# Longer runs of one operand type in split float32 products, and the rounded copies on another engine

## The chip, the cores and the metric

The kernel runs on one core of a Trainium2 chip. The metric is the device time of one execution in microseconds. TensorE (PE in the profile) multiplies, and its weight loads (PEld) have rows of their own; VectorE (DVE), ScalarE (ACT) and GpSimd (POOL) work on tiles, each with an in-order queue; SyncE (SP) issues most transfers (DMA).

## The reference: what is computed

Two decoder layers over 1024 tokens of width 1024, each with a residual and a layer normalization behind it. One input projection per layer gives four groups of columns: main, memory queries, main gate, memory gate.

```python
def mixer_sublayer(x, mem, w_in, w_mem_kv, w_out, main_fn):
    h = x @ w_in
    u_main = h[..., :D_MAIN]            # 1024 columns
    q_mem = h[..., D_MAIN:D_MIX]        # 512 columns, 4 heads of 128
    g_main = h[..., D_MIX:D_MIX + D_MAIN]
    g_mem = h[..., D_MIX + D_MAIN:]
    y_main = main_fn(u_main)
    y_mem = memory_attention(q_mem, mem, w_mem_kv)
    y = concatenate([y_main * silu(g_main), y_mem * silu(g_mem)])
    return y @ w_out
# per layer: x = layer_norm(ALPHA * x + mixer_sublayer(...))
```

In the first layer `main_fn` is a causal pooling with windows of 2, 4, 8 and 16 tokens, followed by a 256x256 matrix for each of four groups. Between the layers one projection of `x` gives keys, values and forget gates. In the second layer `main_fn` is the forgetting attention: 16 heads of 64, logits plus a difference of cumulated log gates, causal softmax. `memory_attention` is an attention with 4 heads over 256 memory tokens. All is float32.

## The kernel before

**The split.** A float32 matrix `a` is kept in three parts: `hi`, `a` rounded to float32r; `lo`, the rest `a - hi` in bfloat16; and `top`, `a` rounded to bfloat16. A product of `a` and `b` is the sum of three products into one accumulator, given by `three` (L153): `hi*hi` in float32r (the profile writes f32), `top*lo` and `lo*top` in bfloat16. `hi_lo` (L156) makes the parts: ScalarE casts `hi` (L159), VectorE subtracts for `lo` (L160), GpSimd copies `top` (L161). Inside the forgetting attention (`low[0]` is true) the weights' three parts are all made by GpSimd (`gp_hi_lo`, L163). `split_w` (L168) issues a weight piece's load on SP and splits it.

**The stages, in time.** The input `X` is loaded transposed and split (`load_x`, L493). Then layer 0: pooling group 0, `mem_kv(0)`, `mem_attention(0)`, pooling groups 1 to 3 (`pool_group`, L521) with parts of the output projection's weights split in between, then the output projection `OutProj.rest` (L436) with the normalization `norm` (L460), which turns each row tile by TensorE transposes (L277) into the next `X`. Layer 1: `mem_kv(1)`, whose projections have those transposes spread between them (`spread`), `mem_attention(1)`, the first pairs' keys, queries and values (`v_first`, L622), the forgetting attention `fox` with projections filled in between its own products, then `OutProj.rest` again.

**Where products are ordered.** `slab` (L193) is the projection of 128 columns for all 1024 tokens: two accumulators (token halves `n`) and two weight pieces `pc` of four 128-row blocks each, 48 products of 512 columns. It is a generator that yields after each product; some are run at once, and others are handed to a `Fill`, which pumps as many columns of them as fit between a stage's own products. `project` in `mem_kv` makes 24 products of 256 columns. The memory attention's `probs` makes three products of 256 columns for each head and row tile. `pool_group` multiplies with the 256x256 matrix. `products` (L413) of `OutProj` makes, for two row tiles `a` and two column halves `nh`, groups of twelve products, for each third `c` of the rows of `w_out`. `v_first` makes 24 products of 272 columns for a row tile. In all of them the innermost loops take the four (or one) float32r products of a piece and then its eight (or two) bfloat16 ones. The order on TensorE is the program's order within `manual_schedule` and is set by the tile scheduler by readiness elsewhere; on the other engines the scheduler sets it, but for instructions marked `keep_in_program_order`.

**Buffers.** Weight pieces rotate through six buffers `w` (two for a piece: `hi`, and `lo` with `top`), raw weights through four `raw`. Slabs accumulate in two banks `pj`; output projections in `pj`, `L`, `T` and `O`. An accumulator is emptied by ScalarE and VectorE: `gate` (L216) by a tanh on ScalarE and a product on VectorE, others by a copy or cast on ScalarE.

Of the kernel before, what the change touches and what calls it, by code (L numbers as in the profile page):

```python
# [18 lines left out]
P = 128  # L19
# [4 lines left out]
NH = 512  # L24
# [48 lines left out]
def trunk_kernel(ctx, tc, x, xT, memT, win, wk, wv0, wv, wmk, wmv, wout, poolw, pscale, lng, lnb, bforget, out):  # L73
# [79 lines left out]
    def three(a, b):  # L153
        return (a.hi, b.hi), (a.top, b.lo), (a.lo, b.top)

    def hi_lo(to, src, pinned=False, top=None):  # L156

        pin = tc.keep_in_program_order if pinned else lambda ins: ins
        pin(nc.scalar.copy(to.hi, src))  # L159
        pin(nc.vector.tensor_tensor(to.lo, src, to.hi.bitcast(F32), ALU.subtract))  # L160
        nc.gpsimd.tensor_scalar(to.top, to.hi.bitcast(F32) if top is None else top, 1.0, 1.0, ALU.mult, ALU.mult)  # L161

    def gp_hi_lo(to, src):  # L163
        nc.gpsimd.tensor_scalar(to.hi, src, 1.0, 1.0, ALU.mult, ALU.mult)
        nc.gpsimd.tensor_tensor(to.lo, src, to.hi.bitcast(F32), ALU.subtract)  # L165
        nc.gpsimd.tensor_scalar(to.top, src, 1.0, 1.0, ALU.mult, ALU.mult)

    def split_w(src_dram, shape):  # L168
        r = raw(shape)
        nc.sync.dma_start(r, src_dram)  # L170
        to = parts_of(wt, shape)
        if low[0]:
            gp_hi_lo(to, r)
        else:
            hi_lo(to, r, top=r)
        return to
# [16 lines left out]
    def slab(pieces_dram, X, evac, banks=("pj", 2)):  # L193

        arrived = isinstance(pieces_dram, list)
        ws = list(pieces_dram) if arrived else [split_w(pieces_dram[0], [P, 4, P])]
        accs = {}
        for n, pc in ((0, 0), (1, 0), (0, 1), (1, 1)) if arrived else ((0, 0), (0, 1), (1, 0), (1, 1)):
            if len(ws) <= pc:
                ws.append(split_w(pieces_dram[pc], [P, 4, P]))  # L200
            if n not in accs:
                accs[n] = ps([P, NH], *banks)
            for i, (a, b) in enumerate(three(ws[pc], X)):
                for k in range(4):
                    kt = pc * 4 + k
                    nc.tensor.matmul(  # L206
                        accs[n], a[:, k, :], b[:, kt, n * NH : (n + 1) * NH],
                        start=kt == 0 and i == 0, stop=kt == KT - 1 and i == 2,
                    )
                    if kt == KT - 1 and i == 2:  # L210
                        evac(slice(n * NH, (n + 1) * NH), accs[n])
                    yield NH
# [8 lines left out]
    def mem_kv(l):  # L221

        ms = [parts_of(T, [P, 4, NMEM]) for _ in range(2)]
        for q in range(4):
            r = raw([P, 2, NMEM])
            nc.sync.dma_start(r, memT[:, 2 * q : 2 * q + 2, :])
            hi_lo(ms[q // 2][:, 2 * (q % 2) : 2 * (q % 2) + 2, :], r, top=r)
        mk = parts_of(MK, [P, MH, NMEM])

        def project(w_dram):  # L230

            acc = ps([P, NH], "pj", 2)[:, :NMEM]
            for pc in range(2):
                for i, (w, m) in enumerate(three(split_w(w_dram[pc], [P, 4, P]), ms[pc])):
                    for k in range(4):
                        nc.tensor.matmul(
                            acc, w[:, k, :], m[:, k, :],
                            start=pc == 0 and k == 0 and i == 0, stop=pc == 1 and k == 3 and i == 2,
                        )
                    if i:  # L240
                        spread()
            return acc
# [54 lines left out]
    def mem_attention(l, X, kv, qtile, ytile, yd):  # L297
# [20 lines left out]
        def probs(i):  # L318
# [54 lines left out]
    class OutProj:  # L373
# [23 lines left out]
        def split(self, upto, pinned=False):  # L397

            while self.n < upto:
                self.fetch(self.n + 1)  # L400
                n = self.n
                kk, nh, j = self.KKS[n // 4], n // 2 % 2, n % 2
                if j == 0:
                    self.ws[nh][kk] = self.wtile(n // 2)
                r = self.raws.pop(0)
                hi_lo(self.ws[nh][kk][j], r, pinned, top=r)
                self.n += 1
# [4 lines left out]

        def products(self, accs, c, ys):  # L413
            for a in range(2):
                for nh in range(2):
                    for i in range(3):
                        for k in range(4):
                            kt = 4 * c + k
                            y, w = three(ys[:, k, a * P : (a + 1) * P], self.ws[nh][kt // 2][kt % 2])[i]
                            nc.tensor.matmul(  # L420
                                accs[a][nh], y, w, start=kt == 8 and i == 0, stop=kt == 7 and i == 2,
                            )
                            yield NH

        def early(self, y, ys):
# [4 lines left out]
            for two in (slice(0, 2), slice(2, 4)):  # L430
                hi_lo(ys[:, two, :], y[:, two, :], True, top=y[:, two, :])
                yield
# [3 lines left out]
        def rest(self, resid, X, dst):  # L436
# [11 lines left out]
            for sp, c in order + [(sp, c) for sp in range(2, ST // 2) for c in (2, 0, 1)]:  # L448
# [3 lines left out]
                nc.sync.dma_start(src, self.yd[c, :, :, sp * 2 * P : (sp + 1) * 2 * P])  # L452
                hi_lo(ys, src, top=src)
                for k, _ in enumerate(self.products(accs[sp], c, ys)):
                    if c != 2 and k % 6 == 5:
                        spread()
# [36 lines left out]
    def load_x(kt, parts=1):  # L493
        r = T(dt=F32)
        for i in range(parts):
            cols = slice(i * S // parts, (i + 1) * S // parts)
            nc.sync.dma_start(r[:, cols], xT[kt, :, cols])
            hi_lo(X[:, kt, cols], r[:, cols], top=r[:, cols])

# [16 lines left out]
    with tc.tile_pool(name="in0", bufs=1) as in0:  # L516
# [4 lines left out]
        def pool_group(g):  # L521
            w = WINDOWS[g]
            pms = []
            for f in (2 * g, 2 * g + 1):
# [15 lines left out]
                pms.append(parts_of(T, [P, S]))  # L540
                hi_lo(pms[-1], pm, top=pm)
# [3 lines left out]
            hi_lo(w2, r, top=r)  # L545
            ys = []
# [30 lines left out]
    with tc.tile_pool(name="in1", bufs=1) as in1:  # L577
# [44 lines left out]
        def v_first():  # L622
# [3 lines left out]
            for kt in range(KT):  # L626
                r = raw([P, FW])
                nc.sync.dma_start(r, wv0[kt // 2, :, kt % 2, :])
                hi_lo(ws[kt // 4][:, kt % 4, :], r, top=r)
            for s in range(ST):  # L630
                acc = ps([P, NH], "pj", 2)
                for kt in range(KT):
                    for i, (u, w) in enumerate(three(X[:, kt, s * P : (s + 1) * P], ws[kt // 4][:, kt % 4, :])):
                        nc.tensor.matmul(acc[:, :FW], u, w, start=kt == 0 and i == 0, stop=kt == KT - 1 and i == 2)
                        yield FW
# [359 lines left out]
```

## Time and profile before

| | us |
|---|---|
| three runs, median (lowest to highest) | 1229.82 (1229.51 to 1230.13) |
| the profiled execution | 1230.34 |
| its span, first to last instruction | 1228.6 |
| TensorE busy | 1202.2 |
| VectorE busy | 839.8 |
| ScalarE busy | 567.3 |
| GpSimd busy | 415.8 |

The granted TensorE clock is 0.997 on average. The span is 1.7 us shorter than the profiled execution's time; the rest lies around it. Rows of the profile name an instruction's line, engine and operation, its output and inputs by the program's names without numbers, the shapes and types, how many were put together, and in brackets or at the end what the engine had waited for. A group's start is the recorded start of its first instruction, and products overlap, so a pitch is taken from starts. `[1.44 <-DVE A L160]` says that TensorE was idle for 1.44 us and that the wait ended with VectorE's write of `A` in line 160.

### The profile page before, as it was taken

To read this page: it belongs to the slowest core of one execution; us is meant where nothing else is said; L and a number is where in the kernel's file an instruction comes from. 1 tells how busy PE (TensorE), PEld (TensorE's weight loads), DVE (VectorE), ACT (ScalarE), POOL (GpSimd) and SP (SyncE) were. 2 spreads that over 40 slices of the span, in tenths; PEclk is the share of its full clock that TensorE was granted. 3 is DMA by queue.
4 is the path that set the end of the run, shared out by engine and by line. 5 is a ranking of instruction groups with operands and counts; after the bars stand their busy time and mean duration, and the time that the engine had idled before them with its cause. 6 is when DMAs were issued, how large, how long until landed. Compare 5 with 4: busy or idle time off the path is not lost. (4 is left out here: it accounts for less than half of the span.)

```text
span 1228.6 us, 20280 instructions
## 1 busy us (share of the span) xinstructions
PE 1202.2 (98%) x7018; PEld 731.9 (60%) x7018; DVE 839.8 (68%) x1853; ACT 567.3 (46%) x1241; POOL 415.8 (34%) x582
## 2 busy tenths in 40 slices
PE   8999999999999999999999999999999999999997
PEld 3566666554555556666675666566666666655553
DVE  7555777585745568457736887878877887775754
ACT  4333662242321123346423776767776777662110
POOL 7233102151421225320203454544445434573110
PEclk9999999999999999999999999999999999999999
DMA  6233544223452334234517778878787989885430
GB/s 223 86 108 93 136 106 144 103 87 112 128 207 103 105 111 154 69 103 100 156 48 185 159 164 187 190 176 184 176 203 165 192 182 228 214 227 180 172 120 35
DMA packets 267414, 178.68 MB, mean 145 GB/s; under 512 B 212272, under 2 KB 225712, under 8 KB 267312
## 3 DMA queue, kind: packets, MB, share of 16 engines
q1 hardware_dynamic: 267312, 177.40, 54.1%
q8 instruction: 55, 0.90, 0.3%
q14 instruction: 47, 0.39, 0.1%
HBM read 94.97 MB, written 22.61 MB: 96 GB/s over the span
## 5 line engine op out<-in xcount | busy, mean ns | idle before, releaser
L206 PE MATMUL pj<-A,w 128*128 128x512 bf16 (+1 forms) x2928 | 691.8, 399 | 7.1 <-DVE A L160 2.0
L206 PEld LDWEIGHTS <-w 128*128 128x128 bf16 x1984 | 170.3, 98 | 236.1 <-issue 65.8
L206 PEld LDWEIGHTS pj<-A,w 128*128 128x128 f32 x976 | 179.2, 189 | 56.1 <-ACT A L159 3.9
L161 POOL TENSOR_SCALAR w<-raw 128x512 bf16<-128x512 f32 x106 | 75.3, 712 | 255.5 <-PE pj L206 163.7
L160 DVE TENSOR_TENSOR w<-raw,w 128x512 bf16<-128x512 f32 x106 | 101.5, 960 | 60.7 <-PE pj L206 43.3
L786 DVE SCALAR_TENSOR_TENSOR P<-T,s,P 128x512 f16<-128x512 f32 x192 | 111.4, 612 | 33.4 <-ACT P L785 32.1
L764 ACT ACTIVATE T<-MK,s 128x512 f32<-128x512 f32 x192 | 111.3, 579 | 43.6 <-DVE s L756 23.4
L785 ACT ACTIVATE P<-T,s 128x512 f16<-128x512 f32 x192 | 103.0, 576 | 43.7 <-ACT T L764 20.7
L420 PEld LDWEIGHTS <-T 128*128 128x128 bf16 x736 | 64.6, 98 | 88.2 <-issue 24.2
L191 PE MATMUL L<-B,B 128*128 128x512 f32 (+3 forms) x384 | 106.2, 383 | 1.1 <-DVE s L756 1.1
L159 ACT CAST w<-raw 128x512 fp32r<-128x512 f32 x106 | 65.3, 618 | 72.0 <-PE pj L206 39.3
L748 POOL TENSOR_SCALAR_AFFINE_SELECT R<-R 128x128 f32<-128x128 f32 x128 | 41.8, 332 | 162.8 <-DVE s L756 127.2
L191 PEld LDWEIGHTS L<-B,B 128*128 128x128 f32 x384 | 71.0, 189 | 21.6 <-DVE s L756 2.6
L756 DVE CUSTOM_DVE_ANT_0 MK<-L,R 128x512 f32<-128x512 f32 (+3 forms) x128 | 72.4, 566 | 11.5 <-PE L L191 7.9
L165 POOL TENSOR_TENSOR w<-raw,w 128x512 bf16<-128x512 f32 x54 | 69.7, 1292 | 25.4 <-PE pj L206 25.1
L161 POOL TENSOR_SCALAR T<-T 128x1024 bf16<-128x1024 f32 x23 | 31.1, 1353 | 123.4 <-PE pj L420 79.3
L159 ACT CAST T<-T 128x1024 fp32r<-128x1024 f32 x23 | 24.0, 1046 | 103.3 <-DMA T<-y0d 53.5
L160 DVE TENSOR_TENSOR T<-T,T 128x1024 bf16<-128x1024 f32 x23 | 34.2, 1487 | 43.2 <-PE pj L420 24.3
L808 PE MATMUL O<-T,V 128*64 128x128 f16 (+1 forms) x1152 | 57.6, 221 | 2.0 <-DMA T<-P 1.9
L808 PEld LDWEIGHTS <-V 128*64 128x64 f16 (+1 forms) x1152 | 50.0, 104 | 15.1 <-issue 7.9
L420 PE MATMUL pj<-B,T 128*128 128x512 bf16 (+1 forms) x192 | 54.4, 399 | 0.0
L420 PE MATMUL L<-B,T 128*128 128x512 f32 (+1 forms) x168 | 48.0, 405 | 1.2 <-POOL T L161 1.2
(230 smaller groups left out, 1748.8 us busy)
## 6 DMA issues: line engine op xcount, KB each, us to landing
raw<-in_win_dram SPq DMA_DIRECT2D x96, 256.0 KB, 2.7
raw<-in_wout_dram SPq DMA_DIRECT2D x40, 256.0 KB, 2.8
B<-B SPq DMA_DIRECT2D x32, 256.0 KB, 4.1
R<-cumd SPq DMA_DIRECT2D x16, 512.0 KB, 4.7
y0d<-Y SPq DMA_DIRECT2D x12, 512.0 KB, 2.9
T<-y0d SPq DMA_DIRECT2D x12, 512.0 KB, 3.8
T<-y1d SPq DMA_DIRECT2D x11, 512.0 KB, 3.9
raw<-in_wmk_dram SPq DMA_DIRECT2D x16, 256.0 KB, 2.6
```

The source lines that it names most:

```text
L159: pin(nc.scalar.copy(to.hi, src))
L160: pin(nc.vector.tensor_tensor(to.lo, src, to.hi.bitcast(F32), ALU.subtract))
L161: nc.gpsimd.tensor_scalar(to.top, to.hi.bitcast(F32) if top is None else top, 1.0, 1.0, ALU.mult, ALU.mult)
L165: nc.gpsimd.tensor_tensor(to.lo, src, to.hi.bitcast(F32), ALU.subtract)
L191: nc.tensor.matmul(acc, a, b, start=i == 0, stop=i == len(terms) - 1)
L206: nc.tensor.matmul(accs[n], a[:, k, :], b[:, kt, n * NH : (n + 1) * NH], start=kt == 0 and i == 0, stop=kt == KT - 1 and i == 2,)
L420: nc.tensor.matmul(accs[a][nh], y, w, start=kt == 8 and i == 0, stop=kt == 7 and i == 2,)
L756: nc.vector.tensor_tensor_reduce(p[:, lo:up], lg, R[:, lo:up], 1.0, top, ALU.add, ALU.min, m[:, n : n + 1])
L764: nc.scalar.activation(e, p[:, lo:up], AF.Exp, bias=top, scale=-1.0, accum_out=sums[:, n, hd % 2, i : i + 1],)
L785: nc.scalar.activation(pair[:, lo:up], e, AF.Copy, scale=r)
L786: nc.vector.scalar_tensor_tensor(pair[:, L + lo : L + up], e, r, pair[:, lo:up], ALU.mult, ALU.subtract)
L808: nc.tensor.matmul(acc[rows, (i % 4) * P : (i % 4) * P + P], v[:, b, 2 * j : 2 * j + (1 if e else 2), :].rearrange("p e d -> p (e d)"), pt ...
```

## The change

The order of products changes so that products of one operand type follow each other in longer runs. In `slab` a half's float32r products of both pieces come in one run of 8, then its 16 bfloat16 ones; the second half takes bfloat16 first, then float32r, so that a run goes on from one half to the next, and from one slab to the next. Where both pieces have arrived (the first pool group) the order goes by pieces. `project` does the same over both pieces and alternates from one call to the next; `v_first` alternates from one row tile to the next over all eight blocks; the memory logits take two heads together; the pooling's small products and the output projection's groups are ordered by type, except the very last group, which is ordered by row tile. Secondly, `hi_lo` makes `top` by a ScalarE copy, with GpSimd kept for the input `X` and for the parts of the output projection that are split inside the forgetting attention (`pinned`, `early`). The weights of the forgetting attention stay on GpSimd.

```diff
+    def gp_copy(to, src):
+        nc.gpsimd.tensor_scalar(to, src, 1.0, 1.0, ALU.mult, ALU.mult)
     def hi_lo(to, src, pinned=False, top=None):
         pin = tc.keep_in_program_order if pinned else lambda ins: ins
         pin(nc.scalar.copy(to.hi, src))
         pin(nc.vector.tensor_tensor(to.lo, src, to.hi.bitcast(F32), ALU.subtract))
-        nc.gpsimd.tensor_scalar(to.top, to.hi.bitcast(F32) if top is None else top, 1.0, 1.0, ALU.mult, ALU.mult)
+        (top or nc.scalar.copy)(to.top, src)
...
# slab
-        for n, pc in ((0, 0), (1, 0), (0, 1), (1, 1)) if arrived else ((0, 0), (0, 1), (1, 0), (1, 1)):
+        high, low_top = (0,), (1, 2)
+        if arrived:
+            order = [(n, pc, part) for pc in range(2) for n, part in ((0, high), (1, high), (1, low_top), (0, low_top))]
+        else:
+            order = [(0, pc, part) for part in (high, low_top) for pc in range(2)]
+            order += [(1, pc, part) for part in (low_top, high) for pc in range(2)]
+        for n, pc, part in order:
...
-            for i, (a, b) in enumerate(three(ws[pc], X)):
+            for i in part:
+                a, b = three(ws[pc], X)[i]
                 for k in range(4):
...
# project
-            for pc in range(2):
-                for i, (w, m) in enumerate(three(split_w(w_dram[pc], [P, 4, P]), ms[pc])):
+            ws = [split_w(w_dram[pc], [P, 4, P]) for pc in range(2)]
+            parts = (1, 2, 0) if len(projected) % 2 else (0, 1, 2)
+            projected.append(acc)
+            for i in parts:
+                for pc in range(2):
+                    w, m = three(ws[pc], ms[pc])[i]
                     for k in range(4):
...
-                    if i:
-                        spread()
+                        if k % 3 == 0:
+                            spread()
...
# memory logits
-                for j in range(2):
+                for n, j in ((0, 0), (0, 1), (1, 1), (2, 1), (1, 0), (2, 0)):
                     h = 2 * hp + j
-                    mm3(lg[:, j, :], three(qs[h][:, i * P : (i + 1) * P], mk[:, h, :]))
+                    a, b = three(qs[h][:, i * P : (i + 1) * P], mk[:, h, :])[n]
+                    nc.tensor.matmul(lg[:, j, :], a, b, start=(n, j) == (0, 0), stop=(n, j) == (2, 0))
...
# OutProj.products
-            for a in range(2):
-                for nh in range(2):
-                    for i in range(3):
+            if apart:
+                order = [(a, nh, part) for a in range(2) for part in (high, low_top) for nh in range(2)]
+            else:
+                order = [
+                    (a, nh, part) for part in ((low_top, high) if c == 0 else (high, low_top))
+                    for a in range(2) for nh in range(2)
+                ]
...
# pooling's matrix
-                    mm3(acc, terms)
+                    mm3(acc, terms[0::3] + terms[1::3] + terms[2::3])
...
# v_first
-                for kt in range(KT):
-                    for i, (u, w) in enumerate(three(X[:, kt, s * P : (s + 1) * P], ws[kt // 4][:, kt % 4, :])):
+                parts = (1, 2, 0) if s % 2 else (0, 1, 2)
+                for i in parts:
+                    for kt in range(KT):
```

More of the change, by code (lines that the diff above doesn't have):

```diff
@@ L171, in split_w @@
         to = parts_of(wt, shape)
[L172 to L175, printed above, removed]
+        (gp_hi_lo if low[0] else hi_lo)(to, r)
         return to
@@ L237, in project @@
                             acc, w[:, k, :], m[:, k, :],
-                            start=pc == 0 and k == 0 and i == 0, stop=pc == 1 and k == 3 and i == 2,
+                            start=(i, pc, k) == (parts[0], 0, 0), stop=(i, pc, k) == (parts[2], 1, 3),
                         )
-                    if i:
-                        spread()
+                        if k % 3 == 0:
+                            spread()
             return acc
@@ L411, in open, with products @@
             return accs[:2], accs[2:]
-        def products(self, accs, c, ys):
-            for a in range(2):
-                for nh in range(2):
-                    for i in range(3):
[L417 to L423, printed above, removed]
+        def products(self, accs, c, ys, apart=False):
+            high, low_top = (0,), (1, 2)
+            if apart:
[5 more added lines that the diff above has]
+                ]
+            for a, nh, part in order:
+                for i in part:
+                    for k in range(4):
+                        kt = 4 * c + k
+                        y, w = three(ys[:, k, a * P : (a + 1) * P], self.ws[nh][kt // 2][kt % 2])[i]
+                        nc.tensor.matmul(
+                            accs[a][nh], y, w, start=kt == 8 and i == 0, stop=kt == 7 and i == 2,
+                        )
+                        yield NH
         def early(self, y, ys):
@@ L430, in early @@
             for two in (slice(0, 2), slice(2, 4)):
-                hi_lo(ys[:, two, :], y[:, two, :], True, top=y[:, two, :])
+                hi_lo(ys[:, two, :], y[:, two, :], True, gp_copy)
                 yield
@@ L452, in rest @@
                 nc.sync.dma_start(src, self.yd[c, :, :, sp * 2 * P : (sp + 1) * 2 * P])
-                hi_lo(ys, src, top=src)
-                for k, _ in enumerate(self.products(accs[sp], c, ys)):
+                hi_lo(ys, src)
+                for k, _ in enumerate(self.products(accs[sp], c, ys, X is None and sp == ST // 2 - 1 and c == 1)):
                     if c != 2 and k % 6 == 5:
@@ L544, in pool_group @@
             w2 = parts_of(MK, [P, 2, 2 * P])
[L545 removed]
+            hi_lo(w2, r)
             ys = []
@@ L628, in v_first @@
                 nc.sync.dma_start(r, wv0[kt // 2, :, kt % 2, :])
[L629 removed]
+                hi_lo(ws[kt // 4][:, kt % 4, :], r)
             for s in range(ST):
                 acc = ps([P, NH], "pj", 2)
[L632 to L634 removed]
+                parts = (1, 2, 0) if s % 2 else (0, 1, 2)
+                for i in parts:
+                    for kt in range(KT):
+                        u, w = three(X[:, kt, s * P : (s + 1) * P], ws[kt // 4][:, kt % 4, :])[i]
+                        nc.tensor.matmul(
+                            acc[:, :FW], u, w, start=kt == 0 and i == parts[0], stop=kt == KT - 1 and i == parts[2],
+                        )
                         yield FW
```

23 lines of the change are left out of this document (12 added, 11 removed).

## The prediction

> **What bounds the kernel now.** I read the page's busy times first, then the chain that ended last, then TensorE's timeline where the chain runs, then every idle time that TensorE's timeline and the waits show. The page, its busy times and two of its groups:
>
> ```profile
> span 1228.6 us, 20280 instructions
> PE 1202.2 (98%) x7018; PEld 731.9 (60%) x7018; DVE 839.8 (68%) x1853; ACT 567.3 (46%) x1241; POOL 415.8 (34%) x582
> ...
> L161 POOL TENSOR_SCALAR w<-raw 128x512 bf16<-128x512 f32 x106 | 75.3, 712 | 255.5 <-PE pj L206 163.7
> ...
> L159 ACT CAST w<-raw 128x512 fp32r<-128x512 f32 x106 | 65.3, 618 | 72.0 <-PE pj L206 39.3
> ```
>
> TensorE is busy 98% of the span; no other engine passes 68%. The time is the sum of the products' pitches (start to start) and about 26 us without a product. So an edit can only pay by a shorter pitch or by a stall that goes, and can only cost by a new stall. The end of the chain shows the pitch; first and last of its evenly spaced groups of twelve:
>
> ```profile
> 1131.59 2.67 PE pj L420 x12
> ...
> 1211.69 2.69 PE pj L420 x12
> ```
>
> These lie 80.10 us and 30 groups apart: 2.670 us for 4 float32r and 8 bfloat16 products, nothing waited for. Inside two such groups (TensorE's timeline, pairs of products):
>
> ```profile
> 1184.39 0.59 PE L420 MATMUL L<-G,T 128*128 128x512 bf16 x2
> ...
> 1185.29 0.63 PE L420 MATMUL pj<-B,T 128*128 128x512 f32 x2
> 1185.76 0.60 PE L420 MATMUL pj<-V,T 128*128 128x512 bf16 x2
> 1186.20 0.59 PE L420 MATMUL pj<-B,T 128*128 128x512 bf16 x2
> ...
> 1187.06 0.59 PE L420 MATMUL pj<-B,T 128*128 128x512 bf16 x2
> 1187.95 0.63 PE L420 MATMUL L<-MK,T 128*128 128x512 f32 x2
> 1188.43 0.60 PE L420 MATMUL L<-B,T 128*128 128x512 bf16 x2
> 1188.87 0.59 PE L420 MATMUL L<-MK,T 128*128 128x512 bf16 x2
> ```
>
> A bfloat16 pair takes 0.43 us (twice the 0.2154 found below). From a bfloat16 pair over the first float32r pair it is 0.90 and 0.89, so that pair takes 0.47 or 0.46: coming into float32r costs nothing beside its slower pitch. The second float32r pair takes 0.47 or 0.48 and the first bfloat16 pair 0.44: the way back costs something. A longer bfloat16 run gives its pitch more sharply:
>
> ```profile
> 24.57 2.96 PE L206 MATMUL pj<-A,w 128*128 128x512 bf16 x13 [1.44 <-DVE A L160]
> 27.37 2.84 PE L206 MATMUL L<-A,w 128*128 128x512 bf16 x12
> ```
>
> 2.80 us over 13 products is 0.2154 us each. With 0.2325 for a float32r one (the mean of 0.47 and 0.46, halved), twelve are 8 x 0.2154 + 4 x 0.2325 = 2.653. Measured 2.670: 0.017 us for each return from float32r to bfloat16. The pairs alone say between 0.01 (0.47+0.44 against 0.47+0.43) and 0.03 (0.48+0.44 against 0.46+0.43).
>
> **The change part by part.** A. *The order.* The count of products stays 7,010. In the two built programs' order on TensorE the returns to bfloat16 fall from 599 to 223: 169 fewer in the projection slabs, 79 in the output projections, 60 in the first values, 48 in the small products, 24 in the memory keys and values; the fill inside the forgetting attention gains a few. 376 x 0.017 = -6.4 us; by the pairs' ends -3.8 to -11.3. A third of them lie between products of 256 or 272 columns, which I price alike. Products into and out of the float16 values products of the forgetting attention also move a little; no quoted row prices that, I take 0 and leave it to the range.
>
> B. *The rounded copies.* 233 of them go from GpSimd to ScalarE: 186 of 128x512, 31 of 128x1024, 16 small ones. At ScalarE's 0.618 for 512 elements, twice that at most for 1024, and 0.4 at a guess for the small ones, that is 115 + 38 + 6 = 159 us more: 567 to about 726 us, 59% of the span. GpSimd gives up at least 233 x 0.712 = 166 us. Neither is near TensorE's 98%, so the mean costs nothing; the cover is that ScalarE's casts of a slab's pieces run while TensorE works through 48 products (four groups, 10.7 us), and if that cover fails in a place, the cast's 0.6 us shows there. The transfers are as many; in a slab the second piece's load is issued on SP 8 products earlier, past nothing that is due sooner.
>
> C. *VectorE next to a quieter GpSimd.* Timelines of VectorE, GpSimd and TensorE at the end of a pool group:
>
> ```profile
> 268.20 0.68 DVE L160 TENSOR_TENSOR B<-raw,B 128x512 bf16<-128x512 f32 x1
> ...
> 274.69 1.09 DVE L160 TENSOR_TENSOR w<-raw,w 128x512 bf16<-128x512 f32 x1
> 275.70 2.11 DVE L160 TENSOR_TENSOR W<-raw,W 128x512 bf16<-128x512 f32 x2
> ```
> ```profile
> 273.66 2.60 POOL L161 TENSOR_SCALAR W<-raw 128x512 bf16<-128x512 f32 x2
> ```
> ```profile
> 278.46 5.63 PE L206 MATMUL pj<-A,w 128*128 128x512 f32 x24 [1.59 <-DVE Y L219]
> 288.58 1.62 PE L191 MATMUL L<-T,MK 128*128 128x512 f32 x6 [0.43 <-DVE Y L560]
> ```
>
> The same subtraction takes 0.68 alone and 1.05 to 1.09 while GpSimd copies. The three from 274.69 on take 3.20 us where 2.04 would do: that alone is 1.16 of the 1.59 us that TensorE then waits for VectorE's gating product, and the stretch before was as crowded. Both stalls end on VectorE and go: -2.0, ends 0 (ScalarE's queue, now with the copies, is late instead) and -2.0. At the head, the 1.44 us at 24.57 also waits for VectorE's subtraction of the input, which GpSimd's copies of weights slow; GpSimd keeps the input's own. I take -1.0, ends 0 and -1.4.
>
> D. *Start of the second layer's memory keys.* One row of busy times by stretch:
>
> ```profile
> 471.00:485.00 14.00, 13.19 (x108) 11.06 (x107) 13.83 (x28) 6.61 (x14) 9.88 (x13) 1.00 0.39 142
> ```
>
> Columns: length, then PE, PEld, DVE, ACT, POOL. VectorE is full, ScalarE has 6.61 us, GpSimd 13 copies. On ScalarE those are about ten at 0.6 and three of half size at 0.4: +7.2, so 13.8 of 14.0 us, in a queue that serves strictly in order transposed input, weights and keys. Both casts and copies are now needed by TensorE within the stretch. TensorE idles 0.8 there; from the queue's order in the changed program I count three places where a cast comes 1.0 to 2.3 us after the product that needs it, less what VectorE saves without GpSimd beside it: +2.5, ends 0 and +4.5.
>
> E. *Start of the last output projection.* Rows of TensorE's timeline, then of the chain:
>
> ```profile
> 1101.37 0.60 PE L420 MATMUL L<-B,T 128*128 128x512 bf16 x2 [1.19 <-POOL T L161]
> ...
> 1123.29 0.74 PE L420 MATMUL L<-R,T 128*128 128x512 f32 x2 [1.33 <-ACT T L159]
> ```
> ```profile
> 1108.87 2.03 POOL V L161 x2
> 1110.89 1.02 POOL G L161
> 1111.91 1.81 POOL G L835 x2
> ...
> 1122.19 1.05 ACT T L159
> ```
>
> The second stall is a chain over GpSimd: the gating product at 1111.91 stands behind copies of weights, its result goes out and comes back, then is cast. Without three copies (3.0 us) ahead of it the chain is early by more than 1.33: -1.3. The copy that the first stall waits for runs on ScalarE after a cast of 1.05, so about 1.0 late against 1.19; but the new order needs the copies 8 products (1.86 us) later. The last row tiles' outputs are evacuated by ScalarE, now behind copies: I keep 0.6 of that stall. -1.9 together, ends -2.5 and +2.0 (three copies of 0.62 ahead of the evacuation, with nothing gained).
>
> Sum: -6.4 - 2.0 - 1.0 + 2.5 - 1.9 = -8.8. Behind the last product (normalization on VectorE and the store) I find nothing that changes. The profiled execution took 1230.3 us, 0.5 above the median of 1229.8; it becomes 1221.5, and a median 1221.0.
>
> **The rivals.** R1, *only the order pays*: the stalls of C and E go and others of the same size come, since ScalarE serves casts, copies, evacuations and exponentials in one queue. For it: D is such a place. Against: outside D its busy share stays near two thirds. 1230.3 - 6.4 = 1223.9, median 1223.4.
>
> R2, *the change does not do what it says*: the 0.017 us belongs to each group's start, or to float32r itself, and long runs do not save it. For it: it is a difference of 0.6% of a group, got from rounded rows. Against: the two slower pairs sit exactly at the border. Then -2.4 by C to E: 1227.9, median 1227.4.
>
> R3, *slower: ScalarE's queue decides in the slabs*. A second piece's float32r cast is now needed 4 products (0.93 us) after the first's, not 12 (2.65 us). If its weight buffer is free only late, release, cast of 0.618 and the copy that stands ahead of it in the queue (0.618) exceed 0.93 by 0.3 us. There are some forty slabs outside the forgetting attention; from 8.8/40 = 0.22 us each on the gain is eaten, at 0.3 it is +12: about 1233.5. For it: the idle of the casts in the page's group ends mostly with a product (39.3 us of 72.0), so buffers are what they wait for. Against: in the changed program's order the buffer taken by the second piece is one that was released some 20 products before.
>
> R4, *slower: narrow float32r products wait for their weights in long runs*. Rows of four memory projections in the first layer and of their weight loads:
>
> ```profile
> 71.29 5.80 PE L236 MATMUL pj<-T,w 128*128 128x256 f32 x48
> 76.84 2.48 PE L206 MATMUL pj<-A,w 128*128 128x512 f32 x10
> ```
> ```profile
> L236 PEld LDWEIGHTS pj<-T,w 128*128 128x128 f32 x128 | 17.9, 190 | 1.9 <-issue 0.4
> ```
>
> A load is recorded with 190 ns; a product of 256 columns would be done in half of 0.2325. If runs of 16 could not overlap loads, each of the 128 products there and 64 of 272 columns would take 0.19 in place of 0.116: +14.2, from 0.046 us each on it eats the gain: 1230.3 - 8.8 + 14.2 = 1235.7. Against: 48 products took 5.55 us, 32 of them at no less than half of 0.2154, which leaves at most 0.131 for each float32r one, in runs of four already; and 128 loads of 190 ns took only 17.9 us, so they overlap. The Trainium skill ("TensorE: Matmul & The Clock Gate", section "Weight-path perf modes") says that the fast weight load is on only where the type is not FP32, and that FP32 gains nothing from it; by that rule this rival is the likelier the longer the run. The trace agrees that the load is longer and, in runs of four, not that it binds; no run here shows sixteen.
>
> **How the numbers follow.** About 2.5 us, 0.2%, is what a measurement of this kernel can tell from no change. Forecast as summed 0.50; R1 0.27; R2 0.08; R3 0.10; R4 0.05. The likeliest, 1221.0, is the time. All of the forecast's and R1's cases are faster, and half of R2's (0.04); the other half is the same, with 0.02 of the partly realized R3 and R4; slower keeps 0.13. Faster 0.81, same 0.06, slower 0.13. The favourable ends of A, C, D and E together would give 1210; half of that way, 1214.5, is the low end. The high end is R2's 1227.4, taken to 1228 for a part of R3; what lies above is about 0.13. The forecast's own range is 1216 to 1225.
>
> **What would show it.** Right: the last chain's groups of twelve or 24 at 0.017 us less for each return saved (24 in 5.31 to 5.32); no stall near 278 and 288 and at the second row tiles' gated input of the last projection; VectorE's subtractions of weights nearer 0.68 than 1.09; ScalarE near 726 us, GpSimd below 260. TensorE's idle after about 465 us near 3 us, on ScalarE's casts. Wrong: idle of 0.2 us or more at every slab's fifth product on ScalarE (R3); narrow float32r products 0.19 apart (R4); chain groups still 2.67 per twelve (R2).

## The result, and the profile after

The changed kernel takes 1218.52 us (median of four runs, 1217.44 to 1219.34) against 1229.97 for the kernel before (1229.51 to 1232.25). The ratio is 0.9903, with a 95% interval of 0.9886 to 0.9920: 11.5 us faster, where 8.8 was forecast. The profiled execution of the changed kernel took 1218.15 us with a span of 1216.4.

The page of the changed kernel, its busy times and three groups, and the subtraction's group in the kernel before:

```profile
span 1216.4 us, 20026 instructions
PE 1193.7 (98%) x7018; PEld 758.7 (62%) x7018; DVE 793.3 (65%) x1853; ACT 697.4 (57%) x1474; POOL 221.0 (18%) x349
...
L163 DVE TENSOR_TENSOR w<-raw,w 128x512 bf16<-128x512 f32 x106 | 75.6, 714 | 83.6 <-PE pj L214 51.5
...
L162 ACT CAST w<-raw 128x512 fp32r<-128x512 f32 x106 | 65.9, 621 | 26.6 <-PE pj L214 14.6
...
L164 ACT CAST w<-raw 128x512 bf16<-128x512 f32 x106 | 65.7, 620 | 18.9 <-PE pj L214 18.2
```
```profile
L160 DVE TENSOR_TENSOR w<-raw,w 128x512 bf16<-128x512 f32 x106 | 101.5, 960 | 60.7 <-PE pj L206 43.3
```

Of the 12.2 us of span, TensorE's busy time gives 8.5 (1202.2 to 1193.7) and its idle time 3.7 (26.4 to 22.7). The first is mostly the order of products (alone it takes off 7.4, as told below), the second is stalls. ScalarE has 130 us more and GpSimd 195 less. VectorE's subtraction for a weight piece takes 0.714 us on average where it took 0.960.

TensorE's timeline at the end of the second pooling group, where the kernel before had waited 1.59 and 0.43 us, and at the head, where it had waited 1.44:

```profile
277.62 5.54 PE L191 MATMUL L<-T,MK 128*128 128x512 f32 x24
282.81 9.57 PE L214 MATMUL pj<-A,w 128*128 128x512 f32 x42
```
```profile
23.29 2.96 PE L214 MATMUL pj<-A,w 128*128 128x512 bf16 x13 [0.83 <-DVE A L163]
```

The first two stalls are gone, the third has become 0.83. What TensorE still waits for (the view of waits; total, count, longest):

```profile
PE O L833 <- DMA T<-P: 2.5, 4, 1.2
PE pj L248 <- ACT w L162: 2.3, 1, 2.3
PE L L191 <- DVE s L781: 2.1, 4, 1.2
PE pj L214 <- DVE B L724: 1.6, 2, 0.8
PE pj L248 <- ACT w L164: 1.4, 2, 0.7
```

Lines 2 and 5 are new: casts for the memory keys of layer 1. No wait of the kernel before for a copy on GpSimd or for a cast of `T` is left.

TensorE executes the same 7,018 products, and up to reordering inside a stage in the same sequence, so the start of the product with a given number can be compared between the traces (to 0.2 us, by which product a stretch begins with). This table gives, for each stretch between two such products, the changed kernel's length less that of the kernel before. The last two columns are the two halves of the change by themselves, which are told of below:

| stretch (start in the kernel before) | changed | order alone | copies alone |
|---|---|---|---|
| 0 to 44.5 us, head | -1.2 | -0.1 | -1.1 |
| to 168, layer 0's memory keys and attention | -1.3 | -0.9 | 0.0 |
| to 216, end of that attention | -1.2 | +4.8 | +5.2 |
| to 260, pooling | -0.2 | -0.2 | 0.0 |
| to 304, the two stalls at 278 and 288 | -3.3 | -1.2 | -2.8 |
| to 460, pooling, output projection | -1.2 | -0.8 | 0.0 |
| to 496, start of layer 1 | +4.4 | +2.0 | +0.1 |
| to 642, memory attention, first values | -2.8 | -1.3 | -0.7 |
| to 1096, forgetting attention | -1.2 | +0.2 | +0.1 |
| to 1132, start of the last projection | -3.6 | -2.6 | -3.0 |
| to the last product | -0.9 | -0.4 | 0.0 |

### The profile page after: what moved, and what is told of

Same layout as the page of the kernel before. It is cut to its first block, busy times and chain, and to the rows that moved or that the text cites. A ratio compares the mean times of both kernels' runs of the same rounds, so it can differ in the third digit from the quotient of the medians.

```text
span 1216.4 us, 20026 instructions
## 1 busy us (share of the span) xinstructions
PE 1193.7 (98%) x7018; PEld 758.7 (62%) x7018; DVE 793.3 (65%) x1853; ACT 697.4 (57%) x1474; POOL 221.0 (18%) x349
## 5 line engine op out<-in xcount | busy, mean ns | idle before, releaser
L214 PE MATMUL pj<-A,w 128*128 128x512 bf16 (+1 forms) x2928 | 684.7, 390 | 3.1 <-DVE B L724 1.6
L214 PEld LDWEIGHTS <-w 128*128 128x128 bf16 x1984 | 182.3, 98 | 223.8 <-issue 23.3
L163 DVE TENSOR_TENSOR w<-raw,w 128x512 bf16<-128x512 f32 x106 | 75.6, 714 | 83.6 <-PE pj L214 51.5
L441 PEld LDWEIGHTS <-T 128*128 128x128 bf16 x736 | 70.7, 98 | 82.9 <-issue 3.7
L157 POOL TENSOR_SCALAR w<-raw 128x512 fp32r<-128x512 f32 x108 | 67.3, 629 | 65.0 <-PE pj L214 59.7
L164 ACT CAST w<-raw 128x512 bf16<-128x512 f32 x106 | 65.7, 620 | 18.9 <-PE pj L214 18.2
L163 DVE TENSOR_TENSOR T<-T,T 128x1024 bf16<-128x1024 f32 x23 | 28.0, 1218 | 52.2 <-ACT T L162 36.9
```

Source lines behind the costliest of these rows:

```text
L157: nc.gpsimd.tensor_scalar(to, src, 1.0, 1.0, ALU.mult, ALU.mult)
L214: nc.tensor.matmul(accs[n], a[:, k, :], b[:, pc * 4 + k, n * NH : (n + 1) * NH], start=seen[n] == 1, stop=seen[n] == 3 * KT,)
L441: nc.tensor.matmul(accs[a][nh], y, w, start=kt == 8 and i == 0, stop=kt == 7 and i == 2,)
```

## The experiments

The kernel before was timed beside each set: medians 1230.3, 1229.7 and 1230.2.

**Each half alone.** `order_only` is the changed kernel with its copies on GpSimd (from `hi`, where the source lies in PSUM); `copies_only` is the kernel before with the new `hi_lo`.

```diff
# order_only
-        (top or nc.scalar.copy)(to.top, src)
+        gp_copy(to.top, to.hi.bitcast(F32) if psum else src)
```
```diff
# copies_only, against the kernel before
-        nc.gpsimd.tensor_scalar(to.top, to.hi.bitcast(F32) if top is None else top, 1.0, 1.0, ALU.mult, ALU.mult)
+        (top or nc.scalar.copy)(to.top, src)
```

> The new order of products with the rounded copies left on GpSimd. Theory: the order and the copies are separate, and the order carries most of the 11.5 us between the two medians (1230.0 and 1218.5). In the trace of the changed kernel a slab of 48 products takes 10.57 us where it took 10.68, so three returns saved are worth 0.11 us, 0.036 each, twice the 0.017 of the prediction; the stretches without a stall together lost about 9.5 us. Then this kernel takes 1220 to 1222: -9.5, the stalls at 278 and 288 us stay (they belong to GpSimd beside VectorE), the 4.7 us lost at the start of layer 1 shrink. Rival: the price is the prediction's 0.017, 6.4 us in all, and the copies did the rest: 1223 to 1225.

> The rounded copies on ScalarE as in the change, the products in the old order. Theory: GpSimd silent beside VectorE takes away the stalls at 278 and 288 us (2.9 us between the two traces) and about 1 at the head, ScalarE's queue at the start of layer 1 costs up to 4.7, the start of the last projection gains up to 3.6: 1227 to 1229 in all, so 1 to 3 us faster than before. Rival 1: these gains come only with the new order; then no change, 1230. Rival 2: in the old order the second piece is needed later, so ScalarE's queue costs nothing at the start of layer 1 and the gain is larger, 1223 to 1225.

Measured: 1230.55 us (ratio 1.0002, 0.9991 to 1.0014) and 1228.10 (0.9980, 0.9970 to 0.9989). The order alone gains nothing, against theory and rival alike; the copies alone gain 2. The second lies in its theory's range, but not by its terms: the start of layer 1 costs it nothing, and the memory attention costs it 5 us. Neither half has the gain, and their sum is 2 us, not 11.5. The busy lines of the two:

```profile
PE 1194.8 (97%) x7018; PEld 757.7 (62%) x7018; DVE 839.8 (68%) x1853; ACT 567.2 (46%) x1241; POOL 422.6 (34%) x582
```
```profile
PE 1204.2 (98%) x7018; PEld 735.1 (60%) x7018; DVE 794.9 (65%) x1853; ACT 696.2 (57%) x1474; POOL 220.2 (18%) x349
```

The order alone does take 7.4 us off TensorE's busy time (1202.2 to 1194.8), but with a span of 1228.5 its idle time is 33.7 instead of 26.4. The copies alone have less idle (span 1226.6, idle 22.4) and 2.0 more busy. The table shows where both lose: 5 us at the end of layer 0's memory attention. TensorE's timeline of the order alone there, ScalarE's and VectorE's, and the row of busy times around the wait's end (the number behind the five engines is the granted clock):

```profile
188.93 0.49 PE L191 MATMUL T<-T,MK 128*128 128x128 f16 x6 [4.14 <-DMA T<-P]
```
```profile
181.44 0.62 ACT L162 CAST MK<-raw 128x512 fp32r<-128x512 f32 x1 [2.25 <-DMA raw<-in_poolw_dram]
181.96 1.70 ACT L351 ACTIVATE P<-P,s 128x256 f16<-128x256 f32 x4
```
```profile
175.80 1.28 DVE L341 TENSOR_REDUCE s<-L 128x2 f32<-128x512 f32 x2
```
```profile
188.00:194.00 6.00, 5.07 (x62) 5.07 (x62) 4.18 (x5) 0.00 (x0) 0.00 (x0) 0.72 0.53 188
```

The values products wait for the last row tile's probabilities, which go through softmax on VectorE and ScalarE and a transposing transfer, while TensorE works off 48 gate products (some 10.7 us). In this chain ScalarE's scaling (181.96) stands behind the cast of the next pooling matrix, and that cast waits 2.25 us for its load. Around the end of the wait of 4.14 us the clock is at 0.72 over 6 us, worth another 6 x 0.28 = 1.7. The copies alone have the same two instructions in the same order, and the kernel before has a small wait at this place:

```profile
181.39 0.62 ACT L162 CAST MK<-raw 128x512 fp32r<-128x512 f32 x1 [2.33 <-DMA raw<-in_poolw_dram]
181.92 1.70 ACT L338 ACTIVATE P<-P,s 128x256 f16<-128x256 f32 x4
...
188.13 0.80 PE L191 MATMUL T<-T,MK 128*128 128x128 f16 x6 [3.28 <-DMA T<-P]
```
```profile
186.59 0.49 PE L191 MATMUL T<-T,MK 128*128 128x128 f16 x6 [0.69 <-DMA T<-P]
```

In the changed kernel the two instructions stand the other way round, and TensorE does not wait:

```profile
171.42 0.69 DVE L341 TENSOR_REDUCE s<-L 128x2 f32<-128x512 f32 x1
...
175.94 1.71 ACT L351 ACTIVATE P<-P,s 128x256 f16<-128x256 f32 x4 [0.50 <-ACT P L345]
177.68 0.62 ACT L162 CAST MK<-raw 128x512 fp32r<-128x512 f32 x1
...
182.16 1.51 PE L191 MATMUL T<-T,MK 128*128 128x128 f16 x24
```

The cast is only one part of the delay. The last row tile's logits begin at 170.17 us in the changed kernel and at 171.63 in the order alone, but VectorE takes their first maximum at 171.42 and at 175.80: 1.25 us behind them against 4.17, since in the order alone it stands behind the previous row tile's work, a subtraction for weights and a gate.

**Taking that cast out of ScalarE's queue.** Both halves again, with the pooling matrices split by GpSimd.

```diff
-            hi_lo(w2, r)
+            gp_hi_lo(w2, r)
```

> The new order with the copies on GpSimd, and in addition the three parts of the pooling's 256x256 matrices made by GpSimd, so that ScalarE no longer casts them. In the trace of the order alone the memory attention of layer 0 loses 4.8 us to the kernel before at one place: a product waits 4.1 us for a transposing transfer, whose source ScalarE scales late, because the cast of the next pooling group's matrix stands ahead of it in ScalarE's queue and waits there for its load; TensorE's products run slower for some us behind that wait. Theory: that is a matter of where the scheduler puts one cast in ScalarE's queue, not of the order of products; without it the order alone gains what its other stages show, 5 to 6 us: 1224.5 to 1225.5. Rival: the wait is for the transfer itself (its queue, its 3.7 us); then nothing changes, 1230.5.

> The copies on ScalarE with the products in the old order, and the pooling's matrices split by GpSimd as in the run beside it. Theory: the same cast costs the copies alone 5.2 us in the memory attention of layer 0; without it they gain what their other stages show (1.0 at the head, 2.8 at 278 and 288 us, 3.0 at the start of the last projection): 1222 to 1223. Rival: nothing changes, 1228.

Measured: 1229.39 (0.9995, 0.9986 to 1.0003) and 1227.54 (0.9979, 0.9968 to 0.9990). Nothing changed, as the rival said, but not for its reason. TensorE's wait in the second kernel, VectorE's last step for the same tile and GpSimd beside it, and that step in the changed kernel:

```profile
187.71 0.49 PE L191 MATMUL T<-T,MK 128*128 128x128 f16 x6 [2.64 <-DMA T<-P]
```
```profile
179.75 3.41 DVE L339 SCALAR_TENSOR_TENSOR P<-P,s,P 128x256 f16<-128x256 f32 x4 [0.63 <-ACT P L338]
```
```profile
180.07 1.39 POOL L157 TENSOR_SCALAR MK<-raw 128x512 fp32r<-128x512 f32 x2 [155.24 <-DMA raw<-in_poolw_dram]
181.43 1.45 POOL L168 TENSOR_TENSOR MK<-raw,MK 128x512 bf16<-128x512 f32 x1
```
```profile
176.48 1.68 DVE L352 SCALAR_TENSOR_TENSOR P<-P,s,P 128x256 f16<-128x256 f32 x4 [0.62 <-ACT P L351]
```

The scaling comes 2.7 us earlier than in the copies alone (179.21 against 181.92), but GpSimd's split of the matrix runs beside VectorE, whose four instructions take 3.41 us where they take 1.68. The edit replaced one delay by another of the same kind as the prediction's step C, and VectorE's late maxima are still there. "It is one cast in ScalarE's queue" does not hold: the chain has hardly any slack, and whatever delays it shows. (In this execution, 1.5 us below its kernel's median, the clock stayed at 1.00, and the stretch is 2.0 us longer than before where the copies alone had 5.2.)

**Giving the chain more time.** One more step in the memory attention's loop, so that more gate products lie between the last logits and the values that need them; on the kernel before as a control, and on both halves.

```diff
-            for t in range(ST + 2):
-                todo = [MVALUES if k in (5, 9) else 0 for k in range(t, ST + 2)]
+            for t in range(ST + 3):
+                todo = [MVALUES if k in (5, 10) else 0 for k in range(t, ST + 3)]
```

> The kernel before, with one more step in the memory attention's loop: the second group of its values products comes one step later, behind one more share of the gates' projections, so that the last row tile's transposing transfer has longer to arrive. A control for the two runs beside it. Theory: this takes away only the 0.7 us wait at 186.6 us (0.85 with what follows it) and perhaps the like one at 601: 1228.3 to 1229.2 where the kernel before takes 1229.8. Rival: the later values delay the pooling groups; then 1230 or more.

> The order alone (copies on GpSimd) with the same additional step. Theory: the order alone loses its gain to one wait in the memory attention of layer 0 (stage 5.1 us longer than before there, with the granted clock at 0.72 behind it); with time for the transfer its other stages' gain of 5.2 us shows, and the 0.85 of the control: 1224 to 1225. Rival: it stays within 1 us of the kernel before, 1229 to 1230, because another wait takes its place.

> The copies alone (old order) with the same additional step. Theory: 5.2 us come back, and the gain of its other stages shows, 7 us against the kernel before: 1222 to 1223.5. Rival: 1227 to 1228 as without the step.

Measured: 1231.37 (1.0007, 0.9998 to 1.0015), 1225.67 (0.9955, 0.9941 to 0.9969) and 1221.77 (0.9931, 0.9917 to 0.9944). The step gives the kernel before nothing, the order alone 4.9 us and the copies alone 6.3. The control goes the way of its rival; the two others end 0.7 above and 0.2 below their theories' ranges. In both, the values' products, now behind 60 gate products, wait no longer for the transfer (the order alone, then the copies alone):

```profile
183.22 1.51 PE L191 MATMUL T<-T,MK 128*128 128x128 f16 x24
```
```profile
183.04 1.50 PE L191 MATMUL T<-T,MK 128*128 128x128 f16 x24
```

So the lost gain was in this wait. With time for the chain the order is worth 4.6 us and the copies 8.5, together 13.0 against the 11.5 of both without the step: they now nearly add. This is the reverse of the prediction's shares (6.4 and 2.4). Both halves together with the step were not run. (The traces of these three kernels lack some hundred records of products each, so they have no column in the table.)

**The price of a return.** The slabs alone back in the old order, and a sequence of products by itself.

```diff
# slabs_4_8: slab as in the kernel before
-            order = [(0, pc, part) for part in (high, low_top) for pc in range(2)]
-            order += [(1, pc, part) for part in (low_top, high) for pc in range(2)]
+        for n, pc in ((0, 0), (1, 0), (0, 1), (1, 1)) if arrived else ((0, 0), (0, 1), (1, 0), (1, 1)):
...
# run_table, in place of the whole computation
+        for run in (1, 2, 4, 8, 16, 32, 64):
+            for _ in range(4):
+                products(low, wide, 8, NH)
+                products(hi, wide, run, NH)
```

> The changed kernel with the projection slabs alone back in the old order (runs of 4 and 8), which gives back 169 returns to bfloat16. Theory: 0.036 us for each, 6.1 us above the changed kernel: 1224.6. Rival: the prediction's 0.017, 2.9 us: 1221.4. In the trace a slab of 48 products should take 10.68 again.

> Only a sequence of products on constants and no part of the reference's computation: four times each, 8 bfloat16 products and then a run of 1, 2, 4, 8, 16, 32 or 64 float32r ones of 512 columns; the same for 1 to 32 with 256 columns. Theory, from the changed kernel's trace: a float32r product takes 0.231 us for the first seven of a run and 0.227 from then on, and the return costs 0.017; so the period is 2.67 us at 4, 5.39 at 16, 9.02 at 32 and 16.29 at 64. Rival (the prediction's): 0.2325 for each and 0.017 for the return; 5.46 at 16, 9.18 at 32, 16.62 at 64. Rival R4 of the prediction: narrow float32r products in runs of 16 or 32 take up to 0.19 each; theory: 0.118 to 0.120 at any length.

The slabs in the old order: 1227.28 us (0.9979, 0.9970 to 0.9987), 8.8 above the changed kernel and above both expectations. This kernel, too, has the long wait in the memory attention (3.3 us, and 6.6 for the stretch against the changed kernel); outside it its trace is 5.9 us longer, near the 6.1 of the theory. But that execution, 1230.62 us, is the slowest of the kernel's twelve; counted from the median, 2.2 us would be left outside the stretch, so this kernel's time does not settle the price. TensorE's timeline of the sequence alone, one execution on constants, shows it directly; two neighbouring runs of each length:

```profile
46.10 1.28 PE L92 MATMUL wide<-hi 128*128 128x512 f32 x4
...
48.77 1.28 PE L92 MATMUL wide<-hi 128*128 128x512 f32 x4
...
71.17 4.00 PE L92 MATMUL wide<-hi 128*128 128x512 f32 x16
...
76.56 4.00 PE L92 MATMUL wide<-hi 128*128 128x512 f32 x16
...
87.35 7.63 PE L92 MATMUL wide<-hi 128*128 128x512 f32 x32
...
96.37 7.63 PE L92 MATMUL wide<-hi 128*128 128x512 f32 x32
```
```profile
139.70 14.88 PE L92 MATMUL wide<-hi 128*128 128x512 f32 x64
...
155.98 14.88 PE L92 MATMUL wide<-hi 128*128 128x512 f32 x64
...
199.40 0.71 PE L92 MATMUL narrow<-hi 128*128 128x256 f32 x4
...
200.76 0.71 PE L92 MATMUL narrow<-hi 128*128 128x256 f32 x4
...
226.73 4.07 PE L92 MATMUL narrow<-hi 128*128 128x256 f32 x32
...
231.44 4.07 PE L92 MATMUL narrow<-hi 128*128 128x256 f32 x32
```

Periods of 2.67, 5.39, 9.02 and 16.28 us at 4, 16, 32 and 64 float32r products, each with 8 bfloat16 ones: the theory's figures to 0.01, not the prediction's. From 32 to 64 a product costs (16.28 - 9.02) / 32 = 0.227 us; with that, and 8 x 0.2158, a return costs 2.67 - 1.726 - 0.907 = 0.037 us at a run of 4 and nearly the same at 32 (9.02 - 1.726 - 7.26 = 0.034). In the trace's single starts rather more than half of it lies in the first seven products of a run, spaced by 0.224 to 0.236 and 0.230 on average, and the rest at the exit. At 256 columns the period is 1.36 us at 4 and 4.71 at 32: (4.71 - 1.36) / 28 = 0.120 us each, so weight loads do not bind as in rival R4. With 0.109 for a bfloat16 one (the spacing of single starts) a narrow return costs 1.36 - 0.872 - 0.48 = 0.01. This rival is refuted up to 32.

**The start of layer 1.** Copies there back on GpSimd (`keys_gpsimd`), transposes four to a projection as before (`spread_4`), and both.

```diff
# keys_gpsimd: for layer 1's memory weights and keys, and for the transposed input
+        if gp:
+            gp_copy(to.top, to.hi.bitcast(F32) if psum else src)
# spread_4: in project
-                        if k % 3 == 0:
-                            spread()
+                    if i:
+                        spread()
```

> The changed kernel with the rounded copies of layer 1's memory weights, of its keys and of the transposed input back on GpSimd; all else as changed. Theory: ScalarE's one queue is what loses 4.7 us there (a product waits 2.3 us for a cast of weights that stands behind copies, two more wait 0.7 for copies), so 3 to 5 us come back: 1213.5 to 1215.5. Rival: the loss comes from the order of the 24 products of a projection and from the transposes that are put between them more densely (twelve instead of four to a projection); then 1218 to 1219.

> The changed kernel with the transposes of the normalized input put between the products of the memory keys as before, four to a projection and not twelve. The start of layer 1 takes 4.4 us longer than before in the changed kernel, 2.0 in the order alone, nothing in the copies alone, and 3.1 with the copies there back on GpSimd. Theory: denser transposes bring their casts and copies into ScalarE's queue in a bunch, ahead of the next weights' casts; with four to a projection 2 to 3.5 us come back: 1215 to 1216.5. Rival: the order of the 24 products itself asks for both weight pieces at once; then 1218 to 1219.

> The changed kernel with both edits at the start of layer 1: its copies back on GpSimd and four transposes to a projection. Alone the first gave 1.3 us back in that stage and the second 2.7, of 4.4. Theory: they take load off the same queue at different instructions, so most of both adds: 1214.5 to 1215.5. Rival: they cure the same wait, and the larger alone counts: 1216 to 1217.

Measured: 1219.61 (0.9914, 0.9902 to 0.9925), 1217.26 (0.9892, 0.9880 to 0.9905) and 1216.57 (0.9886, 0.9872 to 0.9899). The first lies with its rival, the second between its theory and its rival, and both edits together within their rival's 1216 to 1217. The stretch from 460 to 496 us is 3.1 us longer than before with the first, 1.8 with the second, 4.4 in the changed kernel (the first's profiled execution, 1216.81 us, is the fastest of its five). Each edit takes about as much of TensorE's idle time: from 462 to 490 us that is 3.95 us in the changed kernel, 2.72 and 2.78 with one edit, 2.12 with both, and 0.81 before. The two differ by the granted clock, here in the first and in the second:

```profile
470.00:476.00 6.00, 4.68 (x28) 4.46 (x29) 5.13 (x10) 1.92 (x5) 3.63 (x6) 0.72 0.55 168
```
```profile
470.00:476.00 6.00, 5.24 (x43) 4.62 (x43) 5.84 (x12) 5.41 (x12) 0.00 (x0) 1.00 0.57 169
```

Whether the slower clock belongs to the first edit or to that execution, no run tells. The idle time that stays with both edits, 1.3 above the kernel before, is not shown either; it would fit the order of the products, which asks for both weight pieces at once. None of the three kernels is told apart from the changed one by its interval; the last has the lowest median, 2 us below. ScalarE in the changed kernel in front of the longest wait, TensorE behind it, and the clock there:

```profile
467.98 1.07 ACT L162 CAST A<-T 128x512 fp32r<-128x512 f32 x2
469.83 0.59 ACT L164 CAST A<-T 128x512 bf16<-128x512 f32 x1 [0.78 <-DVE A L163]
470.31 0.62 ACT L162 CAST w<-raw 128x512 fp32r<-128x512 f32 x1
```
```profile
470.99 1.65 PE L248 MATMUL pj<-T,w 128*128 128x256 f32 x7 [2.29 <-ACT w L162]
```
```profile
470.00:476.00 6.00, 5.01 (x29) 4.76 (x30) 5.13 (x10) 4.32 (x9) 0.00 (x0) 0.72 0.59 169
```

Three casts of transposed input stand ahead of the weights' cast, and the copy from PSUM waits 0.78 us in the queue for VectorE's subtraction from the same bank. The granted clock is 0.72 over 6 us, 1.7 us more.

## Why the prediction was right, and where it was not

The direction and the size came out, 8.8 forecast and 11.5 measured, but its steps did not each come out, and that the sum lies near is in part luck: A, C and E gave more than their terms, D cost more, and a wait that was not priced was avoided.

- **A, the order (-6.4, bounds -3.8 to -11.3).** Right mechanism, too small a price. The 0.017 us is about the exit alone; a run's first seven products cost as much again, and where every run has four that is hidden in the 0.2325 us taken as their pitch. 244 wide returns at 0.037 and 132 narrow ones at 0.01 are -10.3; busy time shows -8.5, with 1.7 of slower clock at the start of layer 1 against it, and -10.9 in `spread_4` (1191.3 us), where the clock stays at 1.00 there. (Both traces have 7,018 products, not 7,010; no term rests on that.) R2 falls: long runs do save the price. R4 falls with the table of runs: narrow products stand 0.120 us apart, not 0.19. R1, that only the order pays, falls with `copies_only_later`.
- **B, ScalarE's load.** 697 us, not 726: the 31 copies of 1024 columns took 1.04 us each and not 1.24, and records of neighbouring copies overlap, so that busy time grows by less than the sum of the records. Its mean load cost nothing, as said. The cover "in a place" failed where D has it; in a slab only one product waits for a weights' cast, 0.2 us: R3 falls.
- **C, VectorE beside a quieter GpSimd (-3.0).** Right, and slightly small: the stretch with the two stalls gave 3.3 (2.8 with the copies alone) and the head 1.2 (1.1 with the copies alone, but 0.5 in `spread_4`, whose head is the changed kernel's). The Trainium skill has a remark that bears on this ("VectorE: DVE Perf Modes", section "Two Vector instructions with no wait between them", in its rule on hangs): VectorE's second SBUF read interface is shared with GpSimd. That fits 1.68 against 3.41 us for the same four instructions, but no run here shows the interface itself.
- **D, start of layer 1 (+2.5, ends 0 and +4.5).** At its upper end, +4.4, for a reason only half named. The copies alone lose 0.1 there and the order alone 2.0. The prediction overlooked that `project` now puts twelve transposes to a projection where it had four (1.2 us of idle time in `spread_4`), and the slower clock behind the wait of 2.3 us (1.7).
- **E, start of the last projection (-1.9).** -3.6: both stalls are gone, not one and a half. The 0.6 kept for late evacuations was not needed.
- **What was not priced at all.** The wait for transposing transfers in the memory attentions. The kernel before loses 0.7 us to it at 186.6; the changed kernel loses nothing, where VectorE's maxima come early and the cast stands behind the scaling. Each half alone loses 3 to 4 us there and more by the clock. That the forecast came out past this rival, which it had not weighed, is luck: a rival of the other sign at the right place would have been "the last row tile's chain, 10.7 us of cover, no slack".

The low end of the range was not summed right: the favourable ends (-11.3, -2.0, -1.4, 0 and -2.5) give 1213 in place of 1210, and half of that way is 1217, not 1214.5. The measured time lies above it all the same.

What stays open is why the scheduler orders the queues of ScalarE and VectorE as it does in each variant; no run changed that order alone.

## What to carry to other kernels

Where an engine is 98% busy, split an edit's effect into its busy and its idle time: here one half of the change moved the busy time, the other the idle time, and each alone was lost in a wait that both together happened to avoid. A chain through three engines and a transfer that ends just in time is a place to price before any edit that touches a queue on its way. Price a switch of operand type from runs of several lengths, not from one: a cost at entry that spreads over several products looks like their pitch.

## What the runs showed of the hardware

A return from float32r to bfloat16 cost 0.037 us at 512 columns, in part at the exit and in part over the first products after the entry, and 0.01 at 256 columns. An idle TensorE can cost twice: around the end of waits of 4.1 us and of 2.3 us (the latter after one of 0.29) the granted clock was 0.72 over 6 us, and so it was in `keys_gpsimd` behind two waits of 0.92 and 1.32 us; but behind one of 2.64 us it was 1.00. The two short waits, and the row behind the longer one in `copies_only_gpw`:

```profile
469.61 0.38 PE L254 MATMUL pj<-T,w 128*128 128x256 f32 x1 [0.92 <-ACT w L162]
...
471.32 1.46 PE L254 MATMUL pj<-T,w 128*128 128x256 bf16 x6 [1.32 <-DVE w L163]
```
```profile
188.00:194.00 6.00, 6.00 (x85) 5.17 (x83) 5.69 (x7) 0.00 (x0) 0.00 (x0) 1.00 0.49 196
```

The Trainium skill ("TensorE: Matmul & The Clock Gate", section "What's actually happening") says that the clock is halved after an idle window of about 3.4 us, and that the windows run freely. 0.72 over 6 us is what 3.4 us at half the clock would give (6 x 0.28 x 2), and in the order alone the granted clock is 0.50 over the 3.40 us from 189.70, so the halving and its length agree. The idle window does not agree as it stands: no wait of 3.4 us came before it in the changed kernel or in `keys_gpsimd`. That waits of 0.92 and 1.32 us, or one of 2.3, sufficed and one of 2.64 did not is not explained by their length alone; no run here tells how a stretch that is idle in part counts.
